# Four of eight key granules and one of two value halves of the cross-attention's memory move behind the dilated projections

## The chip, the core and the metric

The kernel runs on one core of a Trainium2 chip. The metric is device time of one execution in microseconds (us), taken as the median of several runs. TensorE is called PE below, VectorE DVE, ScalarE ACT, GpSimd POOL; the two queues that issue transfers are those of SyncE (SP) and ACT. Each engine takes its instructions in the order in which the program lists them.

## What is computed

Two transformer blocks follow each other on 512 tokens of width 1024. Only the second block and the two layer norms of the first one matter here:

```python
# first block
x = layer_norm(ALPHA * x + (1 + g1) * mix, ln1_gain, ln1_bias)      # "first layer norm"
h = standardize(x) * (1 + sc2) + sh2
f = conv_glu_ffn(h, w_ffn_up, w_ffn_conv, b_ffn_conv, w_ffn_down)
x = layer_norm(ALPHA * x + (1 + g2) * f, ln2_gain, ln2_bias)        # "second layer norm"
# second block
y = rmsnorm(h, norm_mix_g) @ w_in              # q, k, v of 8 heads, then a and g of the gated convolution
att = dilated_sliding_attention(q, k, v)       # three patterns, 8 heads of 64
u = a * sigmoid(g)
conv = silu(layernorm(conv31(u) + conv_b))     # 31 taps per channel, 512 channels
h = h + concatenate([att, conv]) @ w_out
xq = rmsnorm(h, norm_x_g) @ w_xq
mn = rmsnorm(mem, norm_mem_g)                  # 256 memory tokens
xk = mn @ w_xk                                 # 1024 key features
xv = mn @ w_xv                                 # 1024 value features
h = h + softmax(xq xk^T / 16) xv @ w_xo
h = h + square(relu(rmsnorm(h) @ w_up)) @ w_down
out = rmsnorm(h)
```

The keys and values of the memory depend on nothing but the memory and two weight matrices. They are first read in the cross-attention, behind `w_out`.

## The kernel before

**Products.** Everything is float32. Each operand is split in two parts, `whi` and `wlo` for weights, `hh` and `hl` (or `mnh` and `mnl`, `cath` and `catl`) for activations, and a product is three matmuls: high times high, high times low, low times high. Weights come in granules of 128 by 1024 (half a megabyte): a transfer into `raw` on SP's queue, a rounded copy `whi` on ACT, and the difference `wlo` on DVE. `PLAN` lists the granules in the order of their use, and a ring of five holds the split ones. `phaseB` takes granules whose features end up on the partitions: 24 matmuls over 512 tokens, or over the 256 memory tokens with `N=256`. With `G=g` the first `g` granules are taken in halves: all `g` over the first 256 tokens, then, after the call `mid`, all `g` over the last 256. `phaseA` takes granules whose weights move, and for the two tiles of memory tokens one of its granules is 12 matmuls of 512 columns.

**Norms.** A norm works on token tiles of 128 rows. `to_features` transposes the normalised tiles `xn` on PE (into banks `tr`), evacuates them as `ev` and splits them into `hh` and `hl`. `first_half` and `second` hold the program up until two of the four token tiles have been given out. Where PE would have nothing to do during a layer norm, the kernel before puts memory products: the two halves `c` of `w_xv_2` (four granules each, 512 columns of the values) at the first layer norm, and all eight granules of `w_xk_2` (`XK_LN = 8`) at the second one. Behind the first come the `w_ffn_up` products with `G=3`, behind the second the gate products `ag(e)` of the second block with `G=2`.

**What sets the order.** The Python program emits instructions in the order in which a planner (class `Pace`) thinks that operands are ready. Foreground code calls `phaseA` and `phaseB`; between two groups of matmuls `pump` steps background generators that wait for nothing. A generator that was given with a list of engines is stepped only as long as those are not planned further ahead of PE than its limit. Three background generators matter: `dilated(h)`, one per head (scores, `P`, its transposes `PT`, and for each pair of heads the product `PT,va`, the quotient `ao` and its split `cath`, `catl`); `conv31`, the taps of the convolution on DVE as scalar_tensor_tensor operations on the tiles `cv` (one per channel tile and tap, those that PE does not take), followed by its norm: transposes of `cv`, statistics of `cva`, transposes back, the gate, and the split into `cath` and `catl`; and `to_features` above. When the foreground has nothing left, `until` steps the generators until a condition holds. The order is then fixed in each engine's list. All instructions are issued through one helper, so that the profile shows the same line for all of them; tiles' names tell them apart.

**Around the moved work.** In the second block the foreground runs the gate products, q, k and then v (`ORDER2`), and behind v's the `w_xk_2` granules from `XK_LN` on, an empty range before the change. Then `residual_rms("w_out_2", ...)` starts: its granules of K=256 take the attention's channels first (`CAT[0]` to `CAT[3]`) and the convolution's last (`CAT[4]` to `CAT[7]`).

Of the kernel before, what the change touches and what calls it, by code (L numbers as in the profile page):

```python
# [50 lines left out]
XK_LN = 8  # L51
# [26 lines left out]
# ---------------------------------------------------------------- layouts  # L78
# Weights come as one array of granules [128, 1024], in the order in which they are used:
#   B: 128 output features, all of K=1024      (k, kt, f)     stationary  # L80
#   G: a value and a gate tile of the GLU      (k, 2, kt, f)  stationary
#   A: 256 rows of K, 512 output columns       (k, kt, col)   moving
#   R: 128 rows of w_ada, 1024 columns         (k, col)       not a matmul operand
# [6 lines left out]
def _plan():  # L90
    p = []
# [40 lines left out]
    for c in range(2):  # L132
        A("w_xv_2", range(0, 8, 2), c)
# [20 lines left out]
    for f in range(XK_LN, 8):  # L154
        B("w_xk_2", 128 * f)
    for c in range(2):
        A("w_out_2", OUT_K, c)
# [33 lines left out]
def _tables():  # L191
    """Constants that depend on shapes alone."""
    i = np.arange(128)
# [14 lines left out]
def _pack(inp):  # L208
    """Lays the inputs out; no value is changed."""
# [73 lines left out]
class Pace:  # L283
    """An estimate of when each engine gets to what it is given. It orders the emission only: a piece of
    background work is issued when the tensor engine would find its operands ready."""
# [49 lines left out]
class Engine:  # L335
    """Passes calls on to an engine and tells the pace keeper what they cost."""
# [51 lines left out]
def two_blocks_kernel(ctx: ExitStack, tc: tile.TileContext, x, mem, wg, cols_d, rows_d, b_ada, s5p, wqk, small_d,  # L388
# [44 lines left out]
    # ------------------------------------------------------------ constants  # L433
# [22 lines left out]
    # ------------------------------------------------------------ weight stream  # L456
    class Stream:
# [61 lines left out]
        def _columns(self, j, h, t):  # L519
            """modc[:, 0:2, j] from 128 columns of w_ada for each: the vector engine or the column strips of  # L520
            the tensor engine add up the row tiles, then the tensor engine the partitions."""
# [27 lines left out]
        def _ada(self, part, k, t):  # L549
            """acc[part] += w_ada rows times silu(c), to be summed over the partitions."""  # L550
# [10 lines left out]
        def flush(self, n=0):  # L561
            """The second parts of the granules, when the vector engine need not wait for the first."""
# [13 lines left out]
        def fill(self):  # L576
            """Splits granules ahead of their use, as many as the ring holds and extra ones in slots, once
            the tensor engine has left the room and the other engines have the time."""
# [15 lines left out]
        def get(self, *want):  # L594
            """The two parts of the next granule, each in two halves."""
            while not self.ready:
                self.step()
            while self.late and any(_name(q) == _name(self.late[0][0]) for q in self.ready[0][2]):
                self.flush(len(self.late) - 1)
            e, hi, lo = self.ready.pop(0)  # L600
            assert e[:len(want)] == want, (e, want)
            return hi, lo
# [12 lines left out]
        def rows(self):  # L615
            """Takes the w_ada granules that are next."""
# [5 lines left out]
    # ------------------------------------------------------------ background work  # L622
    # Generators; each yields what its next matrix products need: operands, or a condition on the program.
# [18 lines left out]
    def vacant(tag):  # L642
        """When the next bank of this tag has been read."""
# [6 lines left out]
    def due(g):  # L650
        """When the operands are there; None if the program has not come to them yet."""
# [10 lines left out]
    def top():  # L662
        """Gives the vector engine what the filler has for it."""
# [32 lines left out]
    # ------------------------------------------------------------ products  # L696
    def mmB(p, w, X, n0=0, n1=S, ks=None, nk=None):
        """p[f, tokens] += w[k, f].T @ X[k, tokens] for float32 operands in two exact parts each."""
# [11 lines left out]
    def phaseB(wants, X, evac, G=0, N=S, mid=None):  # L710
        """Feature-major products: one granule gives 128 features of all tokens. The first G granules
        take the first half of the tokens before the second."""
        i = 0
# [22 lines left out]
    def phaseA(name, c, ks, X, tts, evac, off=0):  # L736
        """Token-major products: the activations are stationary, the weights move. Yields per granule."""
# [22 lines left out]
    def tokensA(name, c, ks, X, evac, off=0):  # L760
        """The same, a token tile at a time."""
# [19 lines left out]
    # ------------------------------------------------------------ norms (token-major)  # L781
# [28 lines left out]
    def to_features(xn, tts, X, scale, bias=None):  # L810
        """xn[t][half] normalised tokens -> X[k] (hi, lo) feature-major, times scale (plus bias)."""
# [46 lines left out]
    # ------------------------------------------------------------ modulation  # L858
# [14 lines left out]
    def mod_col(part, i, add_):  # L873
        """The sums of acc[part] over the partitions, features on partitions."""
# [18 lines left out]
    def mod_row(part, name, half, t):  # L893
        """The same on all partitions, features along them."""
# [16 lines left out]
    # ------------------------------------------------------------ first norm  # L911
# [38 lines left out]
    # ------------------------------------------------------------ S5: state space in steps of four tokens  # L950
    # Partitions hold (j, channel) for the four tokens j of a step and the 32 channels of two groups;
    # a state tile holds the 64 complex states of those two groups. With a = exp(lam dt):
# [1276 lines left out]
```

## Time and profile before

| | us |
|---|---|
| median of three runs | 1648.79 (1645.3 to 1649.59) |
| span of the profiled execution | 1648.5 |
| PE busy | 1608.2 (98%) |
| DVE busy | 987.0 (60%) |
| ACT busy | 698.0 (42%) |
| POOL busy | 36.9 (2%) |
| mean granted TensorE clock, share of full | 0.988 |

The span runs from the first to the last instruction of the profiled execution. A matmul's row shows its start and a modelled end; the pitch from one start to the next tells what it costs in a row of many. "Idle before" is time in which the engine stood still ahead of an instruction, and the engine and tile behind the arrow are what ended it. The granted clock is 1.00 at 2.4 GHz and 0.50 at 1.2 GHz. A window's clock between the two is a mix of both.

### The profile page before, as it was taken

The page shows a single profiled execution, that of the slowest core. Times are in us where ns is not written, and L with a number is a line of the kernel's source. Part 1 is how long each engine was busy: PE and PEld are TensorE (multiplying, and loading weights), DVE is VectorE, ACT ScalarE, POOL GpSimd, SP SyncE. Part 2 cuts the span into 40 slices and gives each one's busy share as a digit, 9 for nine tenths or more (in the row PEclk, how much of TensorE's full clock was granted, in tenths as well). Part 3 has the DMA queues.
Part 4 walks back from the last instruction along what each step waited for, and adds up shares of the span by engine and source line. Part 5 has one row for each costly group of instructions (what it writes and reads, how often), then busy time and mean ns, then how long its engine had stood idle before and what let it go on. Part 6 is the DMA issues. An engine that isn't in the chain of part 4 may idle for free.

```text
span 1648.5 us, 20180 instructions
## 1 busy us (share of the span) xinstructions
PE 1608.2 (98%) x7716; PEld 1291.0 (78%) x7716; DVE 987.0 (60%) x1940; ACT 698.0 (42%) x1151; POOL 36.9 (2%) x59
## 2 busy tenths in 40 slices
PE   5999999999999999999999999999999999999998
PEld 3778788778878888888889887557888888888886
DVE  6687768677676536455477878653664533333443
ACT  4454645434345333313336444555644522323231
POOL 1000000000010000000001000000000000000000
PEclk9999999999999999999999999789999999999999
DMA  9422322555714344333254312101311323222221
GB/s 356 137 86 64 115 73 82 185 189 204 247 51 143 101 141 153 98 109 101 93 188 136 109 64 64 39 13 39 128 52 52 128 89 102 90 92 100 89 77 51
DMA packets 63257, 182.66 MB, mean 111 GB/s; under 512 B 7220, under 2 KB 12596, under 8 KB 63160
## 3 DMA queue, kind: packets, MB, share of 16 engines
q1 hardware_dynamic: 55440, 168.25, 31.1%
q10 hardware_dynamic: 7720, 13.12, 2.3%
q8 instruction: 61, 1.00, 0.2%
q14 instruction: 36, 0.29, 0.1%
HBM read 174.00 MB, written 7.34 MB: 110 GB/s over the span
## 4 chain that ended last, share of the span: by engine, by line
PE 68%; DVE 2%; ACT 1%; issue 1%; POOL 0%; DVEq 0%; POOLq 0%; ACTq 0%
PE p L346 68%; DVE mx L346 1%; ACT whi L346 0%; DVE hl L346 0%; ACT PT L346 0%; ACT xn L346 0%; DVE wlo L346 0%; ACT hh L346 0%; ACT P L346 0%; DVE ao L346 0%; DVE st L346 0%; POOL rstd L346 0%; ACT cath L346 0%; DVE P L346 0%; ACT junk L346 0%
## 5 line engine op out<-in xcount | busy, mean ns | idle before, releaser
L346 DVE TENSOR_TENSOR wlo<-raw,whi 128x1024 fp32r<-128x1024 f32 x244 | 297.5, 1224 | 337.2 <-ACT whi L346 336.7
L346 PE MATMUL p<-hh,whi 128*128 128x512 f32 (+1 forms) x1120 | 430.3, 384 | 0.0
L346 PE MATMUL p<-hl,whi 128*128 128x512 f32 (+1 forms) x1120 | 421.9, 377 | 0.6 <-DVE hl L346 0.6
L346 PE MATMUL p<-hh,wlo 128*128 128x512 f32 (+1 forms) x1120 | 422.3, 377 | 0.0
L346 ACT ACTIVATE whi<-raw 128x1024 fp32r<-128x1024 f32 x244 | 256.2, 1055 | 310.9 <-PE p L346 255.2
L346 PEld LDWEIGHTS p<-hh,whi 128*128 128x128 f32 x1120 | 211.0, 188 | 42.8 <-issue 2.6
L346 PEld LDWEIGHTS p<-hl,whi 128*128 128x128 f32 x1120 | 210.9, 188 | 42.8 <-issue 1.7
L346 PEld LDWEIGHTS p<-hh,wlo 128*128 128x128 f32 x1120 | 210.7, 188 | 42.0
L346 PE MATMUL p<-whi,fh 128*128 128x512 f32 x408 | 160.9, 394 | 0.0
L346 PE MATMUL p<-wlo,fh 128*128 128x512 f32 x408 | 160.7, 394 | 0.0
L346 PE MATMUL p<-whi,fl 128*128 128x512 f32 x408 | 160.6, 394 | 0.0
L346 PEld LDWEIGHTS p<-whi,fl 128*128 128x128 f32 x408 | 76.6, 188 | 18.2
L346 PEld LDWEIGHTS p<-whi,fh 128*128 128x128 f32 x408 | 76.6, 188 | 18.1
L346 PEld LDWEIGHTS p<-wlo,fh 128*128 128x128 f32 x408 | 76.6, 188 | 17.8
L346 DVE SCALAR_TENSOR_TENSOR cv<-a,cols,cv 128x511 f32<-128x511 f32 (+14 forms) x106 | 78.3, 740 | 2.1
L346 DVE SCALAR_TENSOR_TENSOR fg<-p,cols,fg 128x511 f32<-128x511 f32 (+1 forms) x44 | 33.0, 749 | 51.0 <-ACT fg L346 50.2
L346 DVE TENSOR_TENSOR mf<-p,mf 128x512 f32<-128x512 f32 x48 | 32.2, 686 | 29.0 <-PE p L346 29.0
L346 ACT ACTIVATE junk<-mf 128x512 f32<-128x512 f32 x32 | 20.2, 630 | 66.0 <-DVE mf L346 66.0
L346 ACT ACTIVATE fg<-p,cols 128x512 f32<-128x512 f32 x22 | 17.1, 779 | 64.8 <-PE p L346 64.8
L346 DVE SCALAR_TENSOR_TENSOR acc<-raw,silu_c,acc 128x512 f32<-128x512 f32 x56 | 38.6, 745 | 2.2 <-DMA raw<-in_wg_dram 2.1
L346 ACT ACTIVATE fh<-sq 128x512 fp32r<-128x512 f32 x32 | 20.2, 632 | 44.9 <-DVE sq L346 44.9
L346 PE MATMUL p<-whi,hh 128*128 128x512 f32 x96 | 38.8, 405 | 0.0
(408 smaller groups left out, 2408.6 us busy)
## 6 DMA issues: line engine op xcount, KB each, us to landing
raw<-in_wg_dram SPq DMA_DIRECT2D x283, 512.0 KB, 3.5
rw<-in_wg_dram SPq DMA_DIRECT2D x32, 256.0 KB, 5.9
x<-in_x_dram SPq DMA_DIRECT2D x8, 256.0 KB, 4.3
xres<-in_x_dram ACTq DMA_DIRECT2D x8, 256.0 KB, 5.7
mn<-mn_dram ACTq DMA_DIRECT2D x8, 256.0 KB, 4.5
out_dram<-mf SPq DMA_DIRECT2D x8, 256.0 KB, 2.1
u_dram<-us ACTq DMA_DIRECT2D x4, 256.0 KB, 4.9
U<-u_dram SPq DMA_DIRECT2D x16, 64.0 KB, 3.7
```

The costliest lines, as they stand in the source:

```text
L346: r = call(*args, **kw)
```

## The change

The diff, with comments that were deleted left out:

```diff
-XK_LN = 8
+XK_LN = 4
...
     for c in range(2):
         A("w_mix_out", range(0, 8, 2), c)
-    for c in range(2):
-        A("w_xv_2", range(0, 8, 2), c)
+    A("w_xv_2", range(0, 8, 2), 0)
...
     for f in range(XK_LN, 8):
         B("w_xk_2", 128 * f)
+    A("w_xv_2", range(0, 8, 2), 1)
...
     drain(*mem_ready)
-    for c in range(2):
-        run(phaseA("w_xv_2", c, range(0, 8, 2), MN, [0, 1], ev_xv(c)))
+    run(phaseA("w_xv_2", 0, range(0, 8, 2), MN, [0, 1], ev_xv(0)))
     first_half()
...
-        phaseB(wants, H2, ev_up, G=0 if n else 3, mid=second)
+        phaseB(wants, H2, ev_up, G=0 if n else 4, mid=second)
...
-        if e < 4:
-            phaseB(ag([e]), H3, ev_ag(e), G=0 if len(U2) + len(VA) + len(QA) else 2, mid=second)
+        if e == 0:
+            phaseB(ag([0, 1]), H3, ev_ag(0), G=4, mid=second)
+        elif e == 1:
+            continue
+        elif e < 4:
+            phaseB(ag([e]), H3, ev_ag(e))
...
     phaseB([("w_xk_2", 128 * i) for i in range(XK_LN, 8)], MN, lambda i, p: ev_xk(i + XK_LN, p), N=256)
+    run(phaseA("w_xv_2", 1, range(0, 8, 2), MN, [0, 1], ev_xv(1)))
     MN.clear()
```

Four `w_xk_2` granules leave the second layer norm and the second half of `w_xv_2` leaves the first one; both now stand behind v's projection, where the dilated attention runs in the background. In return the halved granules become four instead of three behind the first layer norm and four instead of two behind the second. PE's list grows from 7212 to 7284 rows (three more halved granules, 24 matmuls more each), DVE's goes from 1737 to 1731 rows, ACT's stays at 1103.

**PE at the first layer norm.** `xn` are the normalised tiles that are transposed, `p<-whi,mnh` and its like the value products, `p<-hh,whi` the `w_ffn_up` products over half of the tokens. Before, from the last matmuls of the value products' first half on:

```order
L346 MATMUL p_4443<-wlo_4457,mnh_3739 128x512
L346 MATMUL p_4443<-whi_4456,mnl_3743 128x512
L346 MATMUL p_4543<-whi_4478,mnh_3736 128x512
L346 MATMUL p_4543<-wlo_4479,mnh_3736 128x512
L346 MATMUL p_4543<-whi_4478,mnl_3740 128x512
L346 MATMUL p_4543<-whi_4478,mnh_3736 128x512
```

After, from the same matmuls on:

```order
L346 MATMUL p_4443<-wlo_4457,mnh_3739 128x512
L346 MATMUL p_4443<-whi_4456,mnl_3743 128x512
L346 MATMUL p_4543<-small,xn_4314 128x128
L346 MATMUL p_4543<-small,xn_4369 128x128
L346 MATMUL p_4543<-small,xn_4314 128x128
L346 MATMUL p_4543<-small,xn_4369 128x128
L346 MATMUL p_4556<-small,xn_4314 128x128
L346 MATMUL p_4556<-small,xn_4369 128x128
L346 MATMUL p_4556<-small,xn_4314 128x128
L346 MATMUL p_4556<-small,xn_4369 128x128
L346 MATMUL p_4581<-hh_4372,whi_4478 128x256
L346 MATMUL p_4581<-hl_4373,whi_4478 128x256
```

The second half of the values, 48 matmuls with transposes between them, is gone from here; eight transposes and the first `w_ffn_up` granule follow at once. From the last transposes on stand 156 matmuls of 256 columns in a row.

**DVE at the end of the attention.** `cv<-a,cols,cv` are taps of the convolution, `ao` and `catl` belong to a pair of heads, `wlo` to a weight granule, `st` and `mv` to the convolution's norm. Before, from the last taps on (the last pair's `ao` and `catl` come eleven rows further down, behind the statistics):

```order
L346 RECIPROCAL rr_9166<-sm_9156 128x4
L346 SCALAR_TENSOR_TENSOR cv_8215<-a_1473_8009,cols,cv_8215 128x497
L346 TENSOR_TENSOR wlo_9282<-raw_8639,whi_9281 128x1024
L346 TENSOR_TENSOR ao_9310<-p_9301,rs_9299 128x512
L346 TENSOR_TENSOR catl_9313<-ao_9310,cath_9312 128x512
L346 BN_STATS st_9337<-cva_9335 128x6
L346 BN_AGGR mv_9280<-st_9337 128x2
```

After, from the last tap ahead of the last pair's `ao` on:

```order
L346 SCALAR_TENSOR_TENSOR cv_7947<-a_1424_7763,cols,cv_7947 128x497
L346 TENSOR_TENSOR ao_9414<-p_9405,rs_9401 128x512
L346 TENSOR_TENSOR catl_9417<-ao_9414,cath_9416 128x512
L346 SCALAR_TENSOR_TENSOR cv_7947<-a_1424_7763,cols,cv_7947 128x497
L346 SCALAR_TENSOR_TENSOR cv_8167<-a_1438_7852,cols,cv_8167 128x511 x2
L346 SCALAR_TENSOR_TENSOR cv_8167<-a_1438_7852,cols,cv_8167 128x509 x2
L346 SCALAR_TENSOR_TENSOR cv_8167<-a_1438_7852,cols,cv_8167 128x507 x2
L346 SCALAR_TENSOR_TENSOR cv_8167<-a_1438_7852,cols,cv_8167 128x505 x2
L346 SCALAR_TENSOR_TENSOR cv_8167<-a_1438_7852,cols,cv_8167 128x504
L346 TENSOR_TENSOR wlo_9456<-raw_9147,whi_9455 128x1024
L346 SCALAR_TENSOR_TENSOR cv_8167<-a_1438_7852,cols,cv_8167 128x503 x2
L346 SCALAR_TENSOR_TENSOR cv_8167<-a_1438_7852,cols,cv_8167 128x502 x2
```

Before, all taps stand ahead of the last two pairs' `ao`. Now 24 taps and one `wlo` stand behind the last one, and the norm's statistics behind those: ten more taps follow the rows shown.

**PE at the end of the attention.** `p<-PT,va` closes a pair of heads, `p<-whi,cath` and its like are output projection products, `p<-small,cv` the convolution's transposes and `p<-small,cva` the transposes back. Before, the convolution's sixteen `cv` transposes stand ahead of the last pair's `PT,va`, and behind that:

```order
L346 MATMUL p_9409<-PT_9321,va_1611_8816 64x512
L346 MATMUL p_9409<-PT_9393,va_1611_8816 64x512
L346 MATMUL p_9168<-whi_8635,cath_9312 128x512
L346 MATMUL p_9168<-wlo_8636,cath_9312 128x512
L346 MATMUL p_9168<-whi_8635,catl_9313 128x512
L346 MATMUL p_9168<-whi_8635,cath_9420 128x512
L346 MATMUL p_9168<-wlo_8636,cath_9420 128x512
L346 MATMUL p_9168<-whi_8635,catl_9421 128x512
L346 MATMUL p_9430<-small,cva_9335 128x128
L346 MATMUL p_9430<-small,cva_9345 128x128
```

After, 24 output products follow the last pair's `PT,va`, and behind them:

```order
L346 MATMUL p_9282<-wlo_9094,cath_9416 128x512
L346 MATMUL p_9282<-whi_9093,catl_9417 128x512
L346 MATMUL p_9477<-small,cv_7751 128x128
L346 MATMUL p_9477<-small,cv_7760 128x128
L346 MATMUL p_9477<-small,cv_7947 128x128
L346 MATMUL p_9477<-small,cv_8167 128x128
L346 MATMUL p_9487<-small,cv_7751 128x128
```

Of the sixteen `cv` transposes and the sixteen `cva` transposes none stands ahead of the last `PT,va` now, and behind both come the output products of the convolution's channels without anything in between.

## Rows read from the trace of the kernel before

**Rows 1.** Page, parts 1 and 2: busy us by engine, granted clock in 40 slices.

```profile
PE 1608.2 (98%) x7716; PEld 1291.0 (78%) x7716; DVE 987.0 (60%) x1940; ACT 698.0 (42%) x1151; POOL 36.9 (2%) x59
...
PEclk9999999999999999999999999789999999999999
```

**Rows 2.** Windows: stretch, its us, busy us (x count) of PE, PEld, DVE, ACT, POOL, granted clock, DMA.

```profile
475.00:500.00 25.00, 21.09 (x92) 16.39 (x91) 15.92 (x34) 17.92 (x32) 2.71 (x3) 0.93 0.25 78
870.00:902.00 32.00, 32.00 (x257) 31.12 (x256) 23.85 (x48) 22.94 (x46) 3.00 (x5) 1.00 0.42 127
913.00:1037.00 124.00, 124.00 (x555) 97.53 (x553) 101.48 (x191) 55.97 (x107) 0.00 (x0) 1.00 0.24 77
1037.00:1117.00 80.00, 73.47 (x316) 44.19 (x316) 48.07 (x119) 47.57 (x99) 1.02 (x1) 0.81 0.06 20
1050.00:1060.00 10.00, 10.00 (x29) 5.63 (x29) 6.12 (x15) 5.05 (x12) 0.00 (x0) 0.50 0.00 0
```

**Rows 3.** PE timeline, first layer norm: start, us, operation, shapes, [idle before <-releaser].

```profile
484.73 0.50 PE L346 MATMUL p<-whi,mnh 128*128 128x512 f32 x1 [1.61 <-ACT whi L346]
...
489.93 0.63 PE L346 MATMUL p<-whi,mnh 128*128 128x512 f32 x1
...
505.60 0.28 PE L346 MATMUL p<-hh,whi 128*128 128x256 f32 x1
...
523.04 0.39 PE L346 MATMUL p<-hh,whi 128*128 128x512 f32 x1
523.27 0.39 PE L346 MATMUL p<-hl,whi 128*128 128x512 f32 x1
```

**Rows 4.** PE timeline, second layer norm and the first gate products.

```profile
881.01 2.99 PE L346 MATMUL p<-mn,whs 128*128 128x256 f32 x24
883.84 0.40 PE L346 MATMUL p<-mn,whi 128*128 128x256 f32 x2
...
898.33 0.60 PE L346 MATMUL p<-small,xn 128*128 128x128 f32 x4
...
911.95 0.39 PE L346 MATMUL p<-hh,whi 128*128 128x512 f32 x1
```

**Rows 5.** Waits of PE, 1037 to 1127: total us, times, longest.

```profile
PE p L346 <- ACT PT L346: 3.5, 5, 1.7
PE p L346 <- DVE sm L346: 1.3, 2, 0.9
```

**Rows 6.** PE timeline, end of the attention and start of the output projection.

```profile
1106.25 1.14 PE L346 MATMUL p<-small,cv 128*128 128x128 f32 x8 [0.99 <-ACT PT L346]
...
1113.29 3.65 PE L346 MATMUL p<-PT,va 128*64 128x512 f32 x16
...
1119.88 1.03 PE L346 MATMUL p<-small,cva 128*128 128x128 f32 x8
...
1125.74 0.48 PE L346 MATMUL p<-whi,cath 128*128 128x512 f32 x1
```

**Rows 7.** DVE timeline over the same end.

```profile
1097.68 0.71 DVE L346 SCALAR_TENSOR_TENSOR cv<-a,cols,cv 128x497 f32<-128x497 f32 x1
...
1112.36 0.16 DVE L346 SCALAR_TENSOR_TENSOR va<-mv,rstd 128x4 f32<-128x4 f32 x1 [1.22 <-POOL rstd L346]
1117.41 0.69 DVE L346 TENSOR_TENSOR ao<-p,rs 128x512 f32<-128x512 f32 x1 [4.89 <-PE p L346]
1118.80 0.69 DVE L346 TENSOR_TENSOR catl<-ao,cath 128x512 fp32r<-128x512 f32 x1 [0.69 <-ACT cath L346]
...
1123.86 0.69 DVE L346 TENSOR_TENSOR catl<-cv,cath 128x512 fp32r<-128x512 f32 x1 [1.17 <-ACT cath L346]
```

**Rows 8.** ACT timeline over the same end.

```profile
1113.89 2.92 ACT L346 ACTIVATE cva<-cva,va,rstd 128x512 f32<-128x512 f32 x4
```

**Rows 9.** DVE groups, 1037 to 1127: count, busy us, mean ns, idle before.

```profile
L346 DVE SCALAR_TENSOR_TENSOR cv<-a,cols,cv 128x498 f32<-128x498 f32 (+11 forms) x28 | 20.6, 735 | 0.3
...
L346 DVE TENSOR_TENSOR wlo<-raw,whi 128x1024 fp32r<-128x1024 f32 x3 | 3.6, 1223 | 3.4 <-ACT whi L346 3.4
```

## The prediction

> **What bounds the kernel now.** I read the page first: PE is busy for 98% of the span at nearly the full clock everywhere [rows 1], so an edit can gain only where PE stands still or runs at half clock, and loses wherever it makes PE wait anew. The mean of the granted clock over 40 slices shows one dip, and the windows by stage show what it is made of [rows 2]. From 913 to 1037 us (the second block's projections) PE is full at clock 1.00. From 1037 to 1117, where only the dilated attention is left, it is busy for 73.5 of 80 us at a mean clock of 0.81, with stretches such as 1050 to 1060 at 0.50, the 1.2 GHz level. Such a window holds 6.5 us of idle time, and 80 x 0.19 = 15.2 us are lost to the clock: together 21.7 us that other products could fill. The waits name the causes: `PT` of ACT and the row sums `sm` of DVE, short waits of at most 1.7 us [rows 5]. The first layer norm is smaller: 3.9 us idle and 25 x 0.07 = 1.8 us of clock between 475 and 500 [rows 2, 3]. The second one has no gap at all, since eight key granules fill it [rows 2, 4]. The span of this execution, 1648.5, is within 0.3 us of the median, so I add my terms to 1648.5.
>
> **The moved products.** A key granule takes 883.84 - 881.01 = 2.8 us [rows 4], four of them 11.3. A value granule is 12 matmuls at a pitch of 523.27 - 523.04 = 0.23 us [rows 3], four of them 11.1. So 22.4 us of PE work leave the layer norms and go behind v's projection. Splits of weights move with them: eight `whi` on ACT and eight `wlo` on DVE at 1.22 us [rows 9], 9.8 us of DVE time more in the attention, and eight weight transfers on SP's queue; there they are before anything that waits, and the ring of five granules covers them.
>
> **First layer norm.** Before, the second value half fills 489.93 to 505.60, and three halved granules end at 523.04 [rows 3]; a fourth, whole, would take 24 x 0.23 = 5.6 more: 528.6. After, the four halved granules are 192 matmuls, at (523.04 - 505.60 - 0.36 for one group of transposes) / 144 = 0.119 us each. If PE never waited they would begin at 489.9 and with some 2.5 us of transposes end at 515: a gain of 13. But they need `hh` and `hl`, and the last 156 stand behind the last group of transposes, whose banks come free only as ACT and DVE work the groups off. Replaying that by hand with the durations of before, I get this last group at 504.5 and the end at 504.5 + 0.36 + 156 x 0.119 = 523.4: a gain of 5.2, with some eight microseconds of short waits in it where PE had one stretch of values before. After such a gap the clock fell before, too: idle gaps of 1.6 and 0.8 us at 484 to 486 left a clock below 1 in that window [rows 2, 3]. Six to eight gaps in a row could cost 3 to 10 us that way. I take 0, between -5 and +5. Halving a granule costs 48 x 0.119 - 24 x 0.23 = 0.1 us, three times 0.3 in all: nothing here.
>
> **Second layer norm.** Before, two halved gate granules end at 911.95 [rows 4]; two more would take 11.1, to 923.1. After, four key granules are gone and four gate granules are halved. Were the last transposes still at 898.33 [rows 4], the 156 matmuls behind them would end at 898.7 + 18.6 = 917.3; without a wait everything ends 11.3 earlier, at 911.8. My replay lets the last transposes come two to three microseconds earlier, after one wait of 2 us for `hl`: 914.4, that is -8.7. With a little for the clock I take -7, between -9 and 0.
>
> **The attention.** It took 80 us up to the last pair's `PT,va`, which ends at T = 1113.29 + 3.65 = 1116.9 [rows 6]. Now 22.4 us of products come in, the convolution's 16 transposes (2 us) leave for the time behind T, and one more of the 32 score tiles is already done when v's projection ends (about 1 us). Against that the 15.2 us of slow clock go, if PE stays busy enough, and a third of the 6.5 us idle: 22.4 - 3 - 15.2 - 2 = +2. If a dip of the clock stays, +8; if all idle time is filled, -3. So the moved work is here nearly free, which is what the two layer norms' gain of 7 rests on.
>
> **The convolution's end.** This is the term that decides. In the order of before DVE has all taps behind it before the last two pairs; its last `cv` stands at 1097.68, 19 us ahead of T, and it then waits 4.89 us for the last `ao` [rows 7]. In the new order 24 taps and one `wlo` stand behind the last pair's `catl`. Engines take their lists in order, so these cannot start earlier, however long DVE waits for the last `PT,va`. From T on: `ao` and `catl` end at 1118.80 + 0.69, T + 2.6 [rows 7]; 24 taps at 0.735 and a `wlo` at 1.22 [rows 9] make 18.9: T + 21.5. Then the norm: from the `cv` transposes at 1106.25 to `cva` normalised at 1113.89 + 2.92 is 10.6 us [rows 6, 8], of which 1.4 were ACT busy with something else after `va` was there at 1112.52 [rows 7]: 9.2, T + 30.7. From the first `cva` transposes at 1119.88 to the first `catl` of the convolution it is 1123.86 + 0.69 - 1119.88 = 4.7 [rows 6, 7], and I take 5.5, as the second channel tile follows and sixteen transposes precede: T + 36.2. Before, the first output product that needs the convolution started at 1125.74 [rows 6], T + 8.8. So it comes 27 us later, and nothing on PE covers it: of the output projection 24 matmuls (5.6 us) can run, they ran in that time before too, and everything else in PE's list stands behind the `cva` transposes. After idle stretches of some 13 and 6 us PE also starts again at a lower clock. The dip in the first layer norm and the longer ones in the attention bound this by 2 and 9 us [rows 2]; I take 4, nearer the first, as the output products are dense. The tail is +31, between +23 (a shorter tap, a norm that overlaps the last taps) and +38.
>
> A page of the Trainium skill speaks against me here. "Perfetto Trace Analysis", section Optimization Strategy, says that a kernel whose most contended engine changes over time may gain by interleaving those stages; by it the attention, which waits on ACT and DVE, takes in PE-bound products and the sum would be the gain without a tail, the first rival below. The trace agrees with its premise (clock 0.81 in that stage), and no run here shows yet whether the gain remains.
>
> **Sum.** 0 - 7 + 2 + 31 = +26: 1648.5 + 26 = about 1675 us. The bounds of the four terms, added outright, give 1654 to 1700; taken as independent of each other (the root of the squares' sum) 1664 to 1687. Half of them come from replays by hand, so I set the forecast's own range between these: 1658 to 1692.
>
> **Rivals.** *The taps are no tail: faster.* If DVE gets to the taps early enough, for instance because the last pair's `ao` doesn't wait for PE, the tail keeps its T + 8.8, and the rest gives 5.2 + 8.7 + 3 = 17 at best: about 1632. For it speaks that DVE is busy only 60% in all [rows 1] and 60% in the attention [rows 2]; against it that DVE's idle time lies ahead of `ao` [rows 7], and that the order puts 24 taps behind it. It decides at the point where the tail eats the 17 us: the first product of the convolution at T + 26, so about 10 taps behind the last `ao` in place of 24. *It cancels: no difference.* Both layer norms give their 14 us, the attention 3, and the tail is only 17 because the norm overlaps the taps: about 1649. *The clock: worse.* PE stays at 1.2 GHz through the gaps of the first layer norm and well into the output projection, as it did in the attention (a mean of 0.81 over 80 us is 30 us at half); the tail is then +38, the first layer norm +5, the second 0 and the attention +8: 1648.5 + 51 = about 1699. *The change doesn't do what it says.* The instruction lists show the products moved; this has no chance of its own.
>
> **How the numbers follow.** Forecast 0.80, worse by the clock 0.08, no difference 0.06, faster 0.06. What a measurement here can tell from no change is about 0.3%, 5 us. Faster by more than that 0.06, within it 0.06, slower 0.88. The range leaves out the two small cases below, the far end of the one above, and some of the forecast's own ends: 1656 to 1693.
>
> **What would show it.** In the changed profile: PE idle for over 10 us and then again for about 6 behind the last `PT,va`, waiting for `cv` and `cva`; 24 taps in a row on DVE right behind the last `catl`; the window of the attention at a clock of 0.95 or more and hardly longer than 80 us; four halved gate granules done seven to nine microseconds earlier than the same work before. I am wrong in the main point if the last tap starts ahead of the last pair's `ao`, or if PE has products to run while the taps finish; wrong in the smaller ones if the attention's clock stays near 0.8 or the first layer norm loses more than 5 us.

## The result, and the profile of the changed kernel

The changed kernel takes 1666.82 us (1663.91 to 1667.94) beside 1647.96 of the kernel before on the same chip: a ratio of 1.011 with a 95% interval of 1.0094 to 1.0125, slower by 19 us. The forecast was 1675 with a range of 1656 to 1693. The profiled execution's span is 1665.6 us, 17.1 more than before; all stages below are read from it.

The page, busy time by engine and granted clock by slice, against [rows 1]:

```profile
PE 1603.1 (96%) x7788; PEld 1291.4 (78%) x7788; DVE 987.3 (59%) x1940; ACT 698.9 (42%) x1151; POOL 36.8 (2%) x59
...
PEclk9999999999999999999999999987999999999999
```

PE is busy for 5 us less in a span that is 17 us longer, and the dip of the clock has moved from the attention to the end of it (a slice is 41 us).

To see where the time went, five matmuls are read in every profile: the first value product at the first layer norm (A), the first 512-column matmul behind the halved `w_ffn_up` granules, the first key product at the second layer norm, the first 512-column matmul behind the halved gate granules, and the first output product that needs the convolution. Where a kernel has fewer halved granules, the missing ones are added at 5.6 us each (24 matmuls at a pitch of 0.23) and, for the gates, taken off the stage behind, so that each stage holds the same work apart from what was moved. All stages of the runs below are reckoned in the same way:

| stage, us | before | after | difference |
|---|---|---|---|
| A to the end of four `w_ffn_up` granules | 49.3 + 5.6 = 54.9 | 49.6 | -5.3 |
| first key product to the end of four gate granules | 37.5 + 11.1 = 48.6 | 40.1 | -8.5 |
| from there to the first output product of the convolution | 202.7 | 229.5 | +26.8 |
| of it, up to the end of the last `PT,va` | 193.8 | 193.8 | 0.0 |
| of it, behind that | 8.8 | 35.7 | +26.9 |
| from there to the end | 522.8 | 526.3 | +3.5 |

Together with the start of the kernel and the stretch between the layer norms (+0.6) this is the 17.1.

**The layer norms.** PE at the first one (start, us, operation, shapes, idle before and what ended it), where [rows 3] had values up to 505.60:

```profile
485.17 0.50 PE L346 MATMUL p<-whi,mnh 128*128 128x512 f32 x1 [1.69 <-ACT whi L346]
...
490.90 0.66 PE L346 MATMUL p<-small,xn 128*128 128x128 f32 x4 [0.27 <-ACT ev L346]
493.00 0.63 PE L346 MATMUL p<-small,xn 128*128 128x128 f32 x4 [1.44 <-DVE ev L346]
...
496.48 0.39 PE L346 MATMUL p<-hh,whi 128*128 128x256 f32 x1 [1.44 <-ACT hh L346]
...
523.71 0.40 PE L346 MATMUL p<-hh,whi 128*128 128x512 f32 x1
```

Four halved granules are done at 523.71, 49.6 us behind A at 474.09. The waits that the prediction feared are there, at 490.90, 493.00, 496.48 and twice more up to the last group of transposes, but they are few: 4.8 us in all. At the second layer norm, against [rows 4]:

```profile
885.34 0.39 PE L346 MATMUL p<-hl,whi 128*128 128x256 f32 x1 [0.49 <-DVE hl L346]
...
889.78 0.63 PE L346 MATMUL p<-small,xn 128*128 128x128 f32 x4 [1.24 <-DVE hl L346]
...
909.85 0.40 PE L346 MATMUL p<-hh,whi 128*128 128x512 f32 x1
```

Two waits of 0.5 and 1.2 us are all that the four missing key granules leave.

**The attention and its end.** Two windows, up to the last `PT,va` and from there to the convolution's first output product, against [rows 2] (busy us of PE, PEld, DVE, ACT and POOL, then the granted clock):

```profile
1025.00:1103.60 78.60, 76.14 (x431) 52.34 (x431) 45.68 (x102) 50.44 (x100) 0.00 (x0) 1.00 0.25 81
1103.60:1139.30 35.70, 14.33 (x58) 10.21 (x56) 24.49 (x38) 11.67 (x18) 1.01 (x1) 0.72 0.05 15
```

The first one is what the moved products were meant for: the clock is 1.00 where it was 0.81, and PE idles for 2.5 us. In the second PE works for 14.3 of 35.7 us. Its rows, against [rows 6]:

```profile
1100.03 3.65 PE L346 MATMUL p<-PT,va 128*64 128x512 f32 x16
...
1126.12 3.13 PE L346 MATMUL p<-small,cv 128*128 128x128 f32 x13 [15.16 <-ACT cv L346]
1133.38 0.48 PE L346 MATMUL p<-small,cva 128*128 128x128 f32 x1 [4.12 <-ACT cva L346]
...
1139.35 0.80 PE L346 MATMUL p<-whi,cath 128*128 128x512 f32 x1 [0.82 <-ACT cath L346]
```

PE waits 15.2 us for `cv` (the row's releaser is ACT, which scales the last tile by a half once the last tap is in) and 4.1 more for the norm. DVE in that time, against [rows 7]:

```profile
1103.81 0.69 DVE L346 TENSOR_TENSOR ao<-p,rs 128x512 f32<-128x512 f32 x1 [1.10 <-PE p L346]
1105.19 0.69 DVE L346 TENSOR_TENSOR catl<-ao,cath 128x512 fp32r<-128x512 f32 x1 [0.69 <-ACT cath L346]
1105.80 7.66 DVE L346 SCALAR_TENSOR_TENSOR cv<-a,cols,cv 128x497 f32<-128x497 f32 x10
1113.37 1.22 DVE L346 TENSOR_TENSOR wlo<-raw,whi 128x1024 fp32r<-128x1024 f32 x1
1114.51 10.80 DVE L346 SCALAR_TENSOR_TENSOR cv<-a,cols,cv 128x503 f32<-128x503 f32 x14
1127.26 0.69 DVE L346 BATCH_NORM_STATS2 st<-cva 128x6 f32<-128x512 f32 x1 [1.95 <-ACT cva L346]
```

The last pair's `ao` and `catl`, then 10 and 14 taps and a `wlo` between them without a pause from 1105.80 to 1125.31: the order that the instruction list showed. And the clock behind it, three windows from the end of the wait on:

```profile
1130.00:1140.00 10.00, 5.11 (x18) 3.69 (x18) 2.49 (x7) 6.82 (x11) 1.01 (x1) 0.63 0.00 0
1140.00:1150.00 10.00, 9.66 (x31) 7.16 (x30) 4.07 (x8) 4.88 (x7) 0.00 (x0) 0.69 0.00 1
1150.00:1160.00 10.00, 10.00 (x45) 8.09 (x44) 4.89 (x7) 3.79 (x9) 0.00 (x0) 1.00 0.36 107
```

It is still low when the output products begin at 1139.35 and is back within the second window; the first 24 of these products take 9.2 us instead of 5.6 before, and that is the 3.5 us in the last line of the table.

### The profile page after: what moved, and what is told of

It reads as the page before. It is cut to its first block, busy times and chain, and to the rows that moved or that the text cites. A ratio compares the mean times of both kernels' runs of the same rounds, so it can differ in the third digit from the quotient of the medians.

```text
span 1665.6 us, 20330 instructions
## 1 busy us (share of the span) xinstructions
PE 1603.1 (96%) x7788; PEld 1291.4 (78%) x7788; DVE 987.3 (59%) x1940; ACT 698.9 (42%) x1151; POOL 36.8 (2%) x59
## 4 chain that ended last, share of the span: by engine, by line
PE 65%; DVE 4%; ACT 2%; issue 1%; POOL 0%; DVEq 0%; ACTq 0%; POOLq 0%
PE p L346 65%; DVE cv L346 1%; DVE mx L346 1%; DVE hl L346 0%; ACT hh L346 0%; DVE wlo L346 0%; ACT xn L346 0%; ACT whi L346 0%; DVE mf L346 0%; DVE st L346 0%; ACT cva L346 0%; POOL rstd L346 0%; DVE ev L346 0%; ACT junk L346 0%; ACT cv L346 0%
## 5 line engine op out<-in xcount | busy, mean ns | idle before, releaser
L346 DVE TENSOR_TENSOR wlo<-raw,whi 128x1024 fp32r<-128x1024 f32 x244 | 297.1, 1223 | 345.8 <-ACT whi L346 345.4
L346 PE MATMUL p<-hh,whi 128*128 128x512 f32 (+1 forms) x1144 | 436.6, 382 | 1.4 <-ACT hh L346 1.4
L346 PE MATMUL p<-hl,whi 128*128 128x512 f32 (+1 forms) x1144 | 426.7, 373 | 1.2 <-DVE hl L346 1.1
L346 PE MATMUL p<-hh,wlo 128*128 128x512 f32 (+1 forms) x1144 | 426.7, 373 | 0.0
L346 ACT ACTIVATE whi<-raw 128x1024 fp32r<-128x1024 f32 x244 | 256.0, 1054 | 324.7 <-PE p L346 269.0
L346 PEld LDWEIGHTS p<-hh,whi 128*128 128x128 f32 x1144 | 216.0, 189 | 43.4 <-issue 2.6
L346 PEld LDWEIGHTS p<-hl,whi 128*128 128x128 f32 x1144 | 216.1, 189 | 42.5 <-DVE hl L346 1.9
L346 PEld LDWEIGHTS p<-hh,wlo 128*128 128x128 f32 x1144 | 215.7, 189 | 41.3
L346 PE MATMUL p<-whi,fh 128*128 128x512 f32 x408 | 161.0, 395 | 0.0
L346 PE MATMUL p<-wlo,fh 128*128 128x512 f32 x408 | 160.7, 394 | 0.0
L346 PE MATMUL p<-whi,fl 128*128 128x512 f32 x408 | 160.7, 394 | 0.0
L346 PEld LDWEIGHTS p<-whi,fl 128*128 128x128 f32 x408 | 76.6, 188 | 18.2
L346 PEld LDWEIGHTS p<-whi,fh 128*128 128x128 f32 x408 | 76.6, 188 | 18.1 <-DVE facc L346 0.2
L346 PEld LDWEIGHTS p<-wlo,fh 128*128 128x128 f32 x408 | 76.6, 188 | 17.9
L346 DVE SCALAR_TENSOR_TENSOR cv<-a,cols,cv 128x511 f32<-128x511 f32 (+14 forms) x106 | 78.4, 741 | 2.5
L346 DVE SCALAR_TENSOR_TENSOR fg<-p,cols,fg 128x511 f32<-128x511 f32 (+1 forms) x44 | 33.0, 749 | 54.2 <-ACT fg L346 53.4
L346 DVE TENSOR_TENSOR mf<-p,mf 128x512 f32<-128x512 f32 x48 | 32.1, 685 | 29.1 <-PE p L346 29.1
L346 ACT ACTIVATE junk<-mf 128x512 f32<-128x512 f32 x32 | 20.2, 631 | 66.0 <-DVE mf L346 66.0
L346 ACT ACTIVATE fg<-p,cols 128x512 f32<-128x512 f32 x22 | 17.1, 777 | 67.7 <-PE p L346 67.7
L346 DVE SCALAR_TENSOR_TENSOR acc<-raw,silu_c,acc 128x512 f32<-128x512 f32 x56 | 38.6, 744 | 1.9 <-DMA raw<-in_wg_dram 1.9
L346 ACT ACTIVATE fh<-sq 128x512 fp32r<-128x512 f32 x32 | 20.2, 632 | 44.9 <-DVE sq L346 44.9
L346 PE MATMUL p<-whi,hh 128*128 128x512 f32 x96 | 39.0, 406 | 0.0
```

The costliest lines, as they stand in the source:

```text
L346: r = call(*args, **kw)
```

## The experiments

Each is one edit of the changed kernel unless it says otherwise. Ratios are to the kernel before on the same chip.

**e1: the taps ahead of the heads.**

```diff
-CONV_LATE = 2500.0
+CONV_LATE = 3500.0
```

> The changed kernel with one number altered: the planner's limit for the convolution's taps from k's projection on is 3500 ns instead of 2500, so that all taps stand ahead of the last two pairs' ao in DVE's list instead of 24 behind the last one. All products stand where the change put them. Theory (the tail is all that the change costs): the 27 us between the last PT,va and the first output product of the convolution's channels shrink to about 9, the 3.5 us of low clock behind it go too, the layer norms' gains stay: about 1635 us, 1632 to 1640. Rival (DVE's time is what is short in the attention, and taps moved ahead hold up the heads' P by as much as they saved): PT,va ends up to 18 us later and the time is about 1652. Rival (the moved products themselves cost it): no better than 1660.

Measured: 1658.0 us, ratio 1.0055 (1.0039 to 1.0071). PE at the end of the moved products, at the first and the last pair, and at the convolution's first output product:

```profile
1049.65 0.39 PE L346 MATMUL p<-whi,mn 128*128 128x512 f32 x1
...
1053.06 1.51 PE L346 MATMUL p<-PT,va 128*64 128x512 f32 x6
...
1114.17 3.65 PE L346 MATMUL p<-PT,va 128*64 128x512 f32 x16
...
1128.55 0.50 PE L346 MATMUL p<-whi,cath 128*128 128x512 f32 x1 [2.07 <-ACT cath L346]
```

The tail is gone, 10.7 us from the last `PT,va` to the convolution instead of 35.7. But the heads took its place: from the gates' end to the last `PT,va` it is 210.2 us instead of 193.8. The moved products are through at 1049.7, before the first pair has closed, and then the attention is what it was before the change, in a window with idle time and a low clock:

```profile
1057.00:1077.00 20.00, 17.10 (x62) 10.79 (x60) 17.06 (x40) 11.04 (x25) 0.00 (x0) 0.72 0.16 52
```

Of the tail's 27 us 25 are gone and 16 come back in the heads, as the first rival said. That the tail is all that the change costs is refuted; the first rival's own time, 1652, was too low as well.

**e2 and e3: the gate products' grouping.** e2 takes the grouping back, e3 puts it alone into the kernel before:

```diff
-        if e == 0:
-            phaseB(ag([0, 1]), H3, ev_ag(0), G=4, mid=second)
-        elif e == 1:
-            continue
-        elif e < 4:
-            phaseB(ag([e]), H3, ev_ag(e))
+        if e < 4:
+            phaseB(ag([e]), H3, ev_ag(e), G=0 if len(U2) + len(VA) + len(QA) else 2, mid=second)
```

> The changed kernel with the gate products of the second block grouped as before (two halved granules for the first channel tile, the next tile by itself); keys and values stay where the change moved them, and so do their eight splits on DVE. In DVE's list no tap stands behind the last ao here. Theory now (the regrouped gate products delay the start of the convolution, and that pushes the taps behind the heads): no tail; the first layer norm keeps its 5.3, the second loses part or all of its 8.5 because only two halved granules are left to fill the wait, the attention is as long as before: 1636 to 1646, about 1642. Rival (the eight wlo that were moved push the taps back): a tail of some 20 us remains, 1655 to 1665.

> The kernel before with the gate products alone regrouped as in the change: four halved granules for two channel tiles. Nothing else moves. In DVE's list five taps stand behind the last ao. Theory: PE waits for the convolution as in the changed kernel, only shorter: the first output product of the convolution's channels comes at 2.6 + 5 x 0.735 + 9.2 + 5.5 = 21 us behind the last PT,va instead of 8.8, with a microsecond or two of low clock: about 1661, 1655 to 1666. Rival (the moved splits are what delays the taps, the grouping is harmless): 1646 to 1651.

Measured: e2 1657.9 us, 1.0053 (1.0038 to 1.0068); e3 1660.4 us, 1.0073 (1.0056 to 1.009). The end of the attention of e3:

```profile
1107.73 3.65 PE L346 MATMUL p<-PT,va 128*64 128x512 f32 x16
...
1126.42 0.48 PE L346 MATMUL p<-small,cva 128*128 128x128 f32 x1 [5.33 <-ACT cva L346]
...
1132.39 0.50 PE L346 MATMUL p<-whi,cath 128*128 128x512 f32 x1 [0.83 <-ACT cath L346]
```

The convolution's first output product comes 21.0 us behind the last `PT,va` (1107.73 + 3.65), as was worked out from five taps. So the grouping alone, with no product moved, makes the kernel 11 us slower. Four gate granules are halved together, the first channel tile is evacuated later, and the convolution, which lives on these tiles, starts its taps later (at 930.99 instead of 916.00). By its profile, whose span is 9.5 us longer than before, the heads are 7.1 us shorter, the tail is 12.2 longer and the stretch behind it 2.8 longer: what the heads gain the taps lose here, too. Another 2.5 us lie at the first layer norm, which the grouping doesn't touch. e2 shows that the grouping buys nothing either: with two halved granules the second layer norm takes 28.8 + 11.1 = 39.9 us, no more than with four (40.1). But e2 is not at 1642:

```profile
1109.12 5.12 PE L346 MATMUL p<-PT,va 128*64 128x512 f32 x16
1114.17 0.66 PE L346 MATMUL p<-small,cv 128*128 128x128 f32 x4
...
1130.05 0.50 PE L346 MATMUL p<-whi,cath 128*128 128x512 f32 x1 [1.08 <-ACT cath L346]
```

There is no tap behind the last `ao`, yet the last `PT,va` ends at 1114.2, 204.9 us behind the gates, 11 us more than before the change. And a tail of 15.8 us is left instead of 8.8, since the taps end only 4 us ahead of that `ao` and the `cv` transposes still stand behind the heads. The time lies in the rival's range, but only 7 us of it are the tail that the rival named; 11 are in the heads.

**e4: half of the change**, the values alone, with `XK_LN = 8`, the gates as before and four halved granules at the first layer norm.

> Half of the change: the second half of the values behind v's projection and four halved granules at the first layer norm; all eight key granules at the second layer norm and the gate products as before. In DVE's list no tap stands behind the last ao. Theory: the first layer norm gives 5.3 us, the second is as before, the 11.1 us of products fit into the attention's idle and slow time of 21.7 us, so its length changes by -4 to +3, no tail: about 1643, 1640 to 1647. Rival (the gap at the first layer norm costs clock, as the prediction feared): 1648. Rival (products between the heads delay them): 1652 or more.

Measured: 1653.9 us, 1.0039 (1.0024 to 1.0054). The profiled execution took 1658.7 us, 4.8 above the median, so its stages may be too long by that much in all. The first layer norm gives its 5.0 us. From the gates' end to the convolution's first output product it is 211.7 us instead of 202.7, of which 2.1 come up to the last `PT,va` and 7.0 behind it: of 11.1 us of products that came in, 9 show as time, not none:

```profile
1111.41 3.65 PE L346 MATMUL p<-PT,va 128*64 128x512 f32 x16
...
1124.65 0.33 PE L346 MATMUL p<-small,cva 128*128 128x128 f32 x1 [1.34 <-ACT cva L346]
...
1130.89 0.50 PE L346 MATMUL p<-whi,cath 128*128 128x512 f32 x1 [1.09 <-ACT cath L346]
```

The theory fell here, by the median of 1653.9 as by the profile: even half of the products, with the old grouping, is not free. The heads take most of it in, but the taps and the norm behind them come later.

**e6 and e7: which engine's share of the moved work costs.** Both start from e1. e6 leaves the eight moved `wlo` out of DVE, e7 leaves 132 of the 144 moved matmuls out of PE; every other instruction keeps its place.

> e1_taps_early with the wlo of the eight moved granules left out: DVE does not compute them and their matmuls read whi in their place; all other instructions and their order are those of e1. DVE has 9.8 us less work and none of those waits; PE's work is unchanged. Theory (the splits cost): the last PT,va comes 10 to 16 us earlier than in e1 and the time is about 1642, 1636 to 1648. Rival (the products on PE cost): within 3 us of e1's 1658.

> e1_taps_early with 132 of the 144 moved matmuls left out (the first and last of each sum stay): PE has about 20.6 us less work behind v's projection, DVE and ACT do all that they did, in the same order. Theory (the splits cost): the attention is bound by DVE and ACT, so that the time falls by no more than 3 to 8 us: 1650 to 1655. Rival (the products cost): it falls by 15 to 20 us, 1637 to 1643.

Measured: e6 1656.7 us, 1.004 (1.0025 to 1.0055); e7 1657.2 us, 1.0041 (1.0026 to 1.0055). Neither is distinguishable from e1's 1.0055, and the last `PT,va` starts where it did, at 1114.55 in e6 and 1114.44 in e7 (behind the gates' end 1.1 and 2.5 us earlier than in e1):

```profile
1114.55 1.94 PE L346 MATMUL p<-PT,va 128*64 128x512 f32 x8
```

```profile
1114.44 1.94 PE L346 MATMUL p<-PT,va 128*64 128x512 f32 x8
```

Both theories are refuted, and together they say why. In e6 PE is full at 1030 to 1040 and DVE has almost nothing to do; in e7 it is PE that idles, at 1.2 GHz for much of the time. First e6, then e7:

```profile
1030.00:1040.00 10.00, 10.00 (x66) 8.60 (x65) 1.03 (x4) 6.34 (x12) 0.00 (x0) 1.00 0.54 172
```

```profile
1030.00:1040.00 10.00, 6.49 (x21) 3.92 (x19) 4.01 (x10) 7.11 (x15) 0.00 (x0) 0.67 0.43 152
1040.00:1050.00 10.00, 9.15 (x30) 6.82 (x31) 5.98 (x16) 6.62 (x15) 0.00 (x0) 0.50 0.53 160
```

In e7 DVE isn't full either. The waits of DVE and of ACT from 1010 to 1052 (total us, times, longest) show that the two hold each other up:

```profile
ACT P L346 <- DVE sm L346: 14.0, 9, 2.7
DVE wlo L346 <- ACT whi L346: 13.8, 9, 2.3
```

DVE's `wlo` waits for ACT's `whi`, DVE's row sums `sm` for a head stand behind that `wlo`, ACT's `P` waits for these `sm`, and the next `whi` stands behind `P`. In this order the stretch up to 1050 is as long as PE's share of the granules and also as long as this chain of DVE and ACT, so to take away one of the two frees nothing. No run takes both away. And behind it stand the heads with nothing left to fill their waits.

**e5, e8, e12: the moved splits on GpSimd.** The planner charges a split to DVE, and it holds taps and heads back while DVE's planned time is more than the limit ahead of PE's. DVE of the changed kernel, waits between 1015 and 1126 (total us, times, longest):

```profile
DVE wlo L346 <- ACT whi L346: 23.2, 12, 3.2
DVE P L346 <- PE p L346: 5.4, 5, 1.9
```

Twelve `wlo`, six of them of moved granules and six of the output projection, stand 23 us in front of DVE's queue waiting for `whi`, 13 of it the moved ones, beside their own 1.22 us each. So e5 gives the subtraction of the eight moved granules to GpSimd, e8 also takes the gates' grouping back, and e12 moves the splits of the output projection's first half as well. `self.aside` holds the names of the `wlo` in question, and the first two lines are what the planner books for GpSimd:

```diff
-                cost = 520.0 if name == "tensor_tensor" else 100.0 + n
+                cost = (520.0 if n < 256 else 2.2 * n) if name == "tensor_tensor" else 100.0 + n
...
-                tt(lo, t, hi, op=OP.subtract)
+                if _name(lo) in self.aside:
+                    nc.gpsimd.tensor_tensor(lo, t, hi, op=OP.subtract)
+                else:
+                    tt(lo, t, hi, op=OP.subtract)
```

> The changed kernel, where the subtraction that makes wlo of the eight moved granules is taken from DVE and done on GpSimd; the planner knows of it, and by its order no tap stands behind the last ao. Theory (the moved splits, not the moved products, cost the time: in the changed kernel DVE stands still for 23 us in front of 12 wlo, plus 1.22 us each, and both the planner and the chip then run late with the taps): the moved products now fit into the attention, the layer norms' gains of 14 us stay: about 1637 us, 1632 to 1645. Rival (the moved products between the heads are what lengthens the attention): 1650 to 1660. Rival (GpSimd is too slow for 128x1024 and PE waits for wlo): 1660 or more.

> e5 with the gate products grouped as before, so that the convolution starts earlier as well; the second layer norm kept its gain of 8.5 us with that grouping in e2. Theory: taps end earlier than in e5 and nothing else changes: 1632 to 1642, about 1636. Rival (taps that stand ahead of the heads hold up their P on DVE): slower than e5 by 3 to 10 us.

> e8 with the splits for the first column half of the output projection on GpSimd as well. In e8 PE is full at a clock of 1.00 from 1050 to 1130, so nothing is left to gain there: within 3 us of e8, 1636 to 1642. Rival (GpSimd gets to them too late, since it works in order at 2.4 us each): 1643 or more.

Measured: e5 1645.5 us, 0.9976 (0.9966 to 0.9987); e8 1639.1 us, 0.9933 (0.9917 to 0.9949); e12 1640.1 us, 0.9939 (0.9925 to 0.9954). All three beat both kernels, e5 by less than its theory asked for; e12 is not told apart from e8. From e5 to e8, on the same chip, the old grouping of the gates is worth 6.4 us. In e8 the stage behind the gates takes 205.2 us up to the convolution's first output product (at 1116.69), beside 202.7 before: 22.4 us of products came in for 2.5. Six products of the attention's channels stand between the last `cva` transposes and this row:

```profile
1114.86 0.60 PE L346 MATMUL p<-small,cva 128*128 128x128 f32 x4
...
1116.69 0.40 PE L346 MATMUL p<-whi,cath 128*128 128x512 f32 x1
```

**e9: e8's order with the splits on DVE.** GpSimd is only reckoned with, not used. Against e8:

```diff
-                    nc.gpsimd.tensor_tensor(lo, t, hi, op=OP.subtract)
+                    V._eng.tensor_tensor(lo, t, hi, op=OP.subtract)
+                    pace.note("POOL", 2.2 * _free(t), [lo], [t, hi])
```

> e8 with the eight subtractions back on DVE, at the places in the program where e8 gives them to GpSimd; the planner still reckons them as GpSimd's, so that every other instruction of every engine keeps e8's order. Theory A (the order of the lists decides, DVE has time to spare): within 4 us of e8's 1639, 1636 to 1643. Theory B (it is the time that DVE spends on these splits and in front of them, 8 x 1.22 us and some 2 us of waiting each): 1650 to 1660.

Measured: 1641.9 us, 0.9948 (0.9931 to 0.9965). Theory A holds: the gain is 8.2 us beside e8's 10.3, with overlapping intervals, although DVE does all that it does in the changed kernel. The plainest comparison is with e2. Both have the old grouping, the moved products and all splits on DVE, so that every engine has the same instructions, and only the planner's booking and with it their order differ: ratio 1.0053 in e2, 0.9948 in e9, 16 to 17 us for the order alone. Up to the last `PT,va` e9 takes 200.1 us instead of e2's 204.9, and its tail is 8.7 instead of 15.8. PE's last moved product, last `PT,va` and the convolution's transposes back, DVE's last tap, and the window of the attention:

```profile
1100.46 0.39 PE L346 MATMUL p<-whi,mn 128*128 128x512 f32 x1
...
1107.15 3.65 PE L346 MATMUL p<-PT,va 128*64 128x512 f32 x16
1110.74 1.09 PE L346 MATMUL p<-small,cva 128*128 128x128 f32 x8
```

```profile
1069.52 0.73 DVE L346 SCALAR_TENSOR_TENSOR cv<-a,cols,cv 128x497 f32<-128x497 f32 x1
```

```profile
1033.00:1107.00 74.00, 72.95 (x426) 52.80 (x424) 47.61 (x108) 51.96 (x104) 1.02 (x1) 0.99 0.21 71
```

The last tap is there at 1069.5, forty microseconds ahead of the heads' end; the moved products reach up to 1100.5, into the fourth pair of heads; PE is busy for 72.95 of 74 us at a clock of 0.99. In the changed kernel they end with the second pair:

```profile
1070.49 0.40 PE L346 MATMUL p<-whi,mn 128*128 128x512 f32 x1
```

**e10: the 23 taps of the last channel tile left out of the changed kernel.**

> The changed kernel with the 23 taps of the convolution's last channel tile left out on DVE (they are 23 of the 24 that stand behind the last ao); all else is as it was and in the same order. Theory (in the changed kernel's own order these taps are what PE waits for): the last PT,va stays where it was, the first output product of the convolution's channels comes 23 x 0.735 = 17 us earlier, and two of the 3.5 us lost to the clock behind it go too: about 1646, 1643 to 1650. Rival (the norm or ACT holds PE up): no better than 1655.

Measured: 1651.7 us, 1.0008 (0.9999 to 1.0017), 15 us less than the changed kernel by the medians and 17 by the ratios, and just outside the expected range. PE at the last pair and behind it:

```profile
1098.49 3.65 PE L346 MATMUL p<-PT,va 128*64 128x512 f32 x16
...
1110.81 0.77 PE L346 MATMUL p<-small,cv 128*128 128x128 f32 x5 [1.43 <-ACT cv L346]
...
1117.65 0.48 PE L346 MATMUL p<-small,cva 128*128 128x128 f32 x1 [4.68 <-ACT cva L346]
...
1123.63 0.80 PE L346 MATMUL p<-whi,cath 128*128 128x512 f32 x1 [0.82 <-ACT cath L346]
```

From the last `PT,va` (ends at 1102.1) to the first output product it is 21.5 us instead of 35.7. The taps account for 14 us; 17 were expected, and the rest is hidden behind the 24 output products, which run up to 1108.9: ACT's scaling of the last `cv`, at 1110.06, stands behind a `whi` that waits for them. The norm behind the taps, some 13 us beyond the 8.8 of before, stays.

**e11: a control**, the kernel before with the output projection's splits on GpSimd.

> A control: the kernel before, with the subtractions for the first column half of the output projection (the only splits that fall into its attention) on GpSimd. Nothing of the change is in it. Theory (GpSimd helps only because moved splits stood in front of the heads): no difference, 1645 to 1652. Rival (taking splits off DVE is worth something in itself): 1643 or less.

Measured: 1656.2 us, 1.0027 (1.0012 to 1.0042): slightly slower than was expected, not faster. Its profile is 5.6 us longer than before, 2.6 of it at the first layer norm, where nothing was changed, and 2.7 up to the last `PT,va`. In the kernel before, to take splits off DVE gains nothing.

## Why the prediction was right, and where it was off

The direction, the range and the deciding mechanism held: the taps behind the last `ao` make PE wait twice, as read from the order. The forecast was 9 us too high, nearly all of it in the three smaller terms. Point by point:

- **The convolution's end** was forecast at T + 36.2 and came at T + 35.7; with the clock behind it +31 was forecast and 26.9 + 3.5 = 30.4 measured. Each link held: taps done at T + 21.6 (forecast 21.5), PE idle for 15.2 and 4.1 us.
- **The attention** was forecast at +2 and was 0: the moved products were absorbed by idle and slow time, at clock 1.00. But this hangs on the order. In e1 and e2 the stage up to the convolution's first output product grows by 18 us for the 22.4 that came in, in e4 by 9 for 11.1; the changed kernel could absorb them while it let the taps fall behind. The prediction treated the two terms as independent, and they are not: what the heads get in DVE's list, the taps lose.
- **The second layer norm** was forecast at -7 and gave -8.5, what the replay by hand had said (-8.7). The row read as the last transposes of before, 898.33, was not the last: four more stand at 900.90 (`900.90 0.60 PE L346 MATMUL p<-small,xn 128*128 128x128 f32 x4`), and the last group came 5 us earlier, not two to three. The replay's end holds all the same, and the sum went by it.
- **The first layer norm** is the term that was mis-sized: 0 was taken, 5.3 gained, again what the replay had said (5.2). The 3 to 10 us for the clock were not there: the new waits came to 4.8 us instead of eight, and the window 475 to 500 has a clock of 0.89 instead of 0.93 [rows 2], which is one microsecond. This, the second layer norm's 1.5 and the attention's 2 make the 9 us between 26 and 17. Two smaller figures don't come out as written: halving costs 0.2 us a granule by its own sum (not 0.1), and the 9 us that bound the clock behind the tail are not in [rows 2]; the 4 that was taken measured 3.5.
- **A cause named wrongly in passing:** the prediction counted 9.8 us more of DVE time for the moved splits but gave it no price, since the ring of five granules was to cover the moved weights. It covers PE, not DVE: the moved splits wait 13 us in front of DVE's queue, and by e9 against e2 it is the planner's booking of them that puts the taps and heads where they are. And the grouping of the gates was read as a term of the second layer norm alone; e3 is 11 us slower with it and e8 6 us faster than e5 without it, and the rows of e3 show the way, through the convolution's start.
- **The page of the Trainium skill** ("Perfetto Trace Analysis", section Optimization Strategy), by which interleaving stages with different limits may gain, is borne out by e8 and e9, not by the change: the same products gain 8 to 10 us once they are spread over the pairs of heads, with the gates grouped as before.

What stays open: why the planner spends the moved products early, in e1 ahead of the first pair of heads and in e2 ahead of the second one, is argued from the code (DVE's booked time holds the heads back while the foreground goes on), and shown only in so far as e9 differs from e2 in the booking and in nothing else of the work. Three profiles with the first layer norm of before (before, e3, e11) take 54.9, 57.4 and 57.5 us there, so that its gain is 5 to 8 us, not 5.3 to the tenth.

## What to carry to other kernels

When work is moved into a stretch that has idle time, look at every engine's list there, not at the bound engine's gaps alone: what the moved work puts in front of another in-order queue decides whether the gaps can be used. Where a planner sets the order, the booking of the moved work's helpers (here a subtraction of 1.2 us) can be worth more than the work itself; spread the filler over the whole stretch, and let the longest chain that ends there (here taps, norm, transposes) start first. And where a regrouping comes along with a move, cost it by who consumes its results, and try it by itself.

## What the runs showed of the hardware

- The 128x1024 subtraction takes 1.22 us on DVE and 2.4 to 2.9 us on GpSimd (e5, e8). GpSimd has 59 other instructions in the whole kernel, so that little stands behind a subtraction that waits there.
- Two engines that take their lists in order can hold each other up while neither is full: in e7 DVE waits 13.8 us for ACT and ACT 14.0 for DVE within 42 us.
- With PE busy for 72.95 of 74 us between the heads the granted clock stays at 0.99 (e9), where the same heads with 6.5 idle microseconds in 80 had 0.81 [rows 2]; in e7, with the products taken out, it is 0.67 and 0.50.
